# One buffer for the high and low parts of a projection's input, and 512 + 256 column products in place of three of 256

## The chip, the cores and the metric

The kernel runs on one core of one Trainium2 chip. The metric is the time of one execution on the device in microseconds (us). In what follows PE is TensorE (matmuls; PEld its weight loads), DVE is VectorE, ACT is ScalarE, POOL is GpSimd and SP is SyncE, which issues nearly all transfers.

## The reference

Two blocks run one after the other on x, 256 tokens of width 1024, in float32. The first has two layers of a gated mixer and an expert-choice mixture of experts; the change hardly touches it. The second has two layers of this, with `rms` a root-mean-square norm along the tokens' width:

```python
hn = rms(h)
mq, mk, mv, mg, dq, dk, dv, dg, sq, sk, sv, sg = split(hn @ w_in)
#   384 each        256 each         384 each
a = moba(rope(mq), rope(mk), mv)      # 6 heads of 64, causal softmax (one block of 256 keys)
b = diff(rope(dq), rope(dk), dv)      # 8 sub-heads of 32, softmax1 - lam * softmax2, head norm
c = stick(sq, sk, sv)                 # 6 heads of 64, stick-breaking weights, no softmax
h = h + concat(a * silu(mg), b * silu(dg), c * silu(sg)) @ w_out
q = rms(h) @ w_xq                     # 4 heads of 128 against keys and values of a memory
h = h + softmax(q k / sqrt(128)) v @ w_xo
```

## The kernel before

**How a product is made.** Every matrix product of a projection is split: an operand is the sum of a high part (hi, fp32r) and a low part (lo), and the product is hi·wh + hi·wl + lo·wh, summed in PSUM. `wsplit` (L568) makes wh and wl of one weight row block (128 rows): a copy by ACT or DVE into a ring of three wh buffers, a subtraction by DVE or POOL into a ring of three wl buffers. The projection's input stands transposed (features on the partitions) in two SBUF buffers, HH (hi) and HL (lo), each of 8 chunks of 128 features by 256 tokens.

**Two forms of projection.** `linear` (L611) gives tokens on the partitions: the input chunk is the stationary side, wh or wl is streamed (512 or 384 columns). `linear_T` (L626) gives features on the partitions: a 128-column piece of wh or wl is stationary and the 256 tokens of HH or HL are streamed. For each of 8 row blocks kc and each chunk c of 128 output features it issues three matmuls of 256 columns (wh·hi, wl·hi, wh·lo); two chunks share one PSUM bank. In the second block `linear_T` is called five times in a layer: for the stick attention's q, k and g (`stick_in`, L1882, three chunks each), for the moba attention's g (`moba_in`, L1770, three chunks) and for the cross attention's q (`xattn`, L1949, four chunks). That is 16 chunks by 8 row blocks in a layer, 256 such triples in both. (`mem_kv` calls it too, with inputs in G0 and G1; those calls stay as they are.)

**Buffers.** PSUM has eight banks: `lin` three, `aux` four, `acc` one. Scores, transposes and sums of the attentions use `aux`; projections use `lin`. Scratch in SBUF: S2 (five), S4 (three).

**Order of work.** The program is first recorded as a list of operations with their dependencies (`Plan.add`); `Plan.order` then schedules the whole list with fixed costs of its own for each operation and latency, forwards and backwards in eight rounds, and picks the engine where two are allowed (`either`: copies on ACT or DVE, subtractions on DVE or POOL). Each engine then runs its instructions strictly in the order issued. Since everything is issued from one line (`Plan.issue`), all rows of the profile carry the line L461, and the tiles tell them apart. A change of buffers or of operations in `linear_T` therefore moves instructions all over the second block.

**A layer of the second block** issues, in the program's text: norm and transposes into HH, HL (`between_blocks` in layer 0, `norm2` after), `stick_in` (q, k, v, g), `diff_in` (two blocks of 512 columns by `linear`), `stick`, `moba_in` (three blocks of 384 columns by `linear`, then g), `diff`, `moba`, `w_out` by `linear` from XC (hi) and KC (lo), then `xattn`. The schedule runs the attentions of one kind between the projections of the next.

Of the kernel before, what the change touches and what calls it, by code (L numbers as in the profile page):

```python
# [12 lines left out]
F32 = mybir.dt.float32  # L13
F32R = mybir.dt.float32r
# [3 lines left out]
ALU = mybir.AluOpType  # L18
# [18 lines left out]
C_END = C_ROPE + 512  # L37


BUFS = {"W": (2048, 4), "HH": (2048, 1), "HL": (2048, 1), "OH": (2048, 1), "OL": (2048, 1), "Z0": (2048, 1), "Z1": (2048, 1),  # L40
        "QA": (2048, 1), "QB": (1024, 1), "KX": (2048, 1), "KC": (2048, 1), "G0": (2048, 1), "G1": (2048, 1), "XC": (2048, 1),
        "DFT": (2048, 1), "S4": (1024, 3), "S2": (512, 5), "wh": (512, 3), "wl": (512, 3), "gb": (1024, 1),
        "M": (2304, 1),
# [1 line left out]
        "lin": (512, 3), "aux": (512, 4), "acc": (512, 1)}  # L45

PARTS = {"Vx": (0, 512), "Vc": (512, 512), "ropeg": (1024, 512), "kf": (1536, 384), "pr1": (1920, 192), "pr2": (2112, 192)}
SHARED = {"PT": ("Vx", "Vc", "kf")}

MIXED = ("HH", "HL", "OH", "OL", "QA", "QB", "KX", "KC", "DFT", "G0", "G1", "XC")  # L50
PSUM_TAGS = ("lin", "aux", "acc")

O_LF, O_GQ, O_GK, O_GV, O_WQ, O_WK, O_WV, O_GATE = 0, 256, 768, 896, 1024, 1280, 1408, 1536
# [86 lines left out]
class Buffer:  # L140


    def __init__(self, make, row=0, after=None):
        self.make, self.row, self.after = make, row, after
        self.tile = None
        self.seen, self.ops = [], []
# [321 lines left out]
class Net:  # L468
    def __init__(self, tc, A, out, ctx, dbg=None, stop=None):
        self.tc, self.nc, self.A, self.out = tc, Plan(tc.nc), A, out  # L470
        self.dbg, self.stop = dbg or {}, stop
        self.sp = ctx.enter_context(tc.tile_pool(name="g", bufs=1))
        self.pp = ctx.enter_context(tc.tile_pool(name="pp", bufs=1, space=bass.MemoryType.PSUM))
        self.bufs, self.turn = {}, {}
        self.wring, self.wonce = ["W"], []
        self.wseq = 0
        self.loads = []
        self.bg, self.bgrate = [], 0


    def slot(self, tag):

        if tag in SHARED:
            i = self.turn[tag] = self.turn.get(tag, -1) + 1
            return self.slot(SHARED[tag][i % len(SHARED[tag])])
        if tag in PARTS:
            o, n = PARTS[tag]
            return self.slot("M")[:, o:o + n]
        n, count = BUFS[tag]
        i = self.turn.get(tag, 0)  # L490
        self.turn[tag] = i + 1
        psum = tag in PSUM_TAGS
        key = f"{tag}{i % count}"
        old = self.bufs.get(key)
        if old is None or tag in MIXED:
            pool, name = self.pp if psum else self.sp, f"{key}_{i}"
            old = self.bufs[key] = Buffer(lambda: pool.tile([128, n], F32, name=name, tag=key), 0 if psum else n, old)
        return View(old, bass.AP(self.A["consts"].tensor, 0, [[n, 128], [1, n]]))

    def t(self, shape, dt, tag):  # L500
        n = math.prod(shape[1:])
        v = self.slot(tag)[:shape[0], :n]
        if dt != F32:
            v = v.bitcast(dt)
        if len(shape) > 2:
            k = "abcde"[:len(shape) - 1]
            v = v.rearrange("p (%s) -> p %s" % (" ".join(k), " ".join(k)), **dict(zip(k, shape[1:])))
        return v
# [21 lines left out]
    def wslot(self):  # L530
        if self.wonce:
            tag = self.wonce.pop(0)
        else:
            tag = self.wring[self.wseq % len(self.wring)]
            self.wseq += 1
        return self.t([128, BUFS[tag][0] // 1024 * 1024], F32, tag)

    def wload(self, src, k0, nk, c0, ncol):
        t = self.wslot()
# [83 lines left out]
            for t in range(2):  # L623
                evac(t, n0 - c0, ps[t][:, :width])

    def linear_T(self, hi, lo, src, c0, evac, K=8, n=4):  # L626

        nc = self.nc
        ps = [self.lin_ps() for _ in range((n + 1) // 2)]
        ws = self.split_stream(src, [c0], K, list(range(K)), 128 * n)  # L630
        for kc in range(K):
            wh, wl = next(ws)
            for c in range(n):
                o = ps[c // 2][:, (c % 2) * 256:(c % 2) * 256 + 256]
                cs = slice(c * 128, c * 128 + 128)
                st = kc == 0 and c % 2 == 0
                nc.tensor.matmul(o, wh[:, cs], hi[:, kc, :], start=st, stop=False, skip_group_check=True)
                nc.tensor.matmul(o, wl[:, cs], hi[:, kc, :], start=False, stop=False, skip_group_check=True)
                nc.tensor.matmul(o, wh[:, cs], lo[:, kc, :], start=False, stop=kc == K - 1, skip_group_check=True)
        for c in range(n):  # L640
            evac(c, ps[c // 2][:, (c % 2) * 256:(c % 2) * 256 + 256])

    def evac(self, out, ps):
        self.copy(out, ps)
# [61 lines left out]
        self.to_T(xn, a, b, hi, lo)  # L706

    def hilo(self, a, b):
        return self.t([128, 8, 256], F32R, a), self.t([128, 8, 256], F32R, b)

    def sub_scaled(self, out, f, hi, scale):
# [1170 lines left out]
    def stick_in(self, hi, lo, w_in, r, R, vg):  # L1882
        q = self.t([128, 2, 3, 256], F32R, "QA")
        k = self.t([128, 2, 3, 256], F32R, "KX")
        v = vg[:, :768].rearrange("p (t c) -> p t c", t=2)
        g = vg[:, 768:].rearrange("p (c q) -> p c q", c=3)

        def split(dst, scale):
            def ev(c, ps):
                f = self.t([128, 256], F32, "S2")  # L1890
                self.nc.vector.scalar_tensor_tensor(out=f, in0=ps, scalar=scale, in1=R, op0=ALU.mult, op1=ALU.mult)
                self.split_evac(dst[:, 0, c], dst[:, 1, c], f)
            return ev
        self.linear_T(hi, lo, w_in, 2560, split(q, 0.125), n=3)
        self.linear_T(hi, lo, w_in, 2944, split(k, 1.0), n=3)
        self.linear(hi, lo, w_in, 3328, 384, lambda t, n0, ps: self.scaled(v[:, t], ps, r[:, t:t + 1]), width=384)
        self.linear_T(hi, lo, w_in, 3712, lambda c, ps: self.times(g[:, c], ps, R), n=3)
        return q, k, v, g

    def stick(self, q, k, v, g, mh, ml):  # L1900
# [168 lines left out]
```

## Time and profile before

| | |
|---|---|
| median of three runs | 2073.83 us (2080.98, 2073.66, 2073.83) |
| the profiled execution's own time | 2074.04 us |
| its span in the trace | 2072.3 us |
[...]
| PE busy | 1834.5 us (89% of the span) |
| DVE / ACT / POOL busy | 891.8 / 850.4 / 305.0 us |
| HBM traffic | 606.63 MB read, 294 GB/s over the span |
| the second block | from about 1683 us to the end |

The span is measured from the first to the last instruction; the execution's own time is 1.7 us more. The first block and its experts fill the first 1683 us; in the stretches with the experts' weights the transfers run at 421 GB/s. In the second block TensorE is busy nearly all the time.

### The profile page before, as it was taken

How to read it: one execution, taken by the hardware profiler on the slowest of the kernel's cores; microseconds unless marked ns; L12 is line 12 of the kernel's file. 1: busy time of each engine (PE TensorE's matmuls, PEld its weight loads, DVE VectorE, ACT ScalarE, POOL GpSimd, SP SyncE). 2: the span in 40 equal slices, each digit the busy share in tenths (PEclk: the TensorE clock that was granted, in tenths of full speed). 3: DMA queues.
4: the chain of work that ended last, by engine and by line, in shares of the span. 5: the costliest groups of instructions: out<-in, count | busy, mean ns of one | idle time of the engine just before them, and what ended most of it. 6: DMA issues, size and time to landing. Idle time of an engine off the chain costs nothing.

```text
span 2072.3 us, 29481 instructions
## 1 busy us (share of the span) xinstructions
PE 1834.5 (89%) x11564; PEld 1137.8 (55%) x11564; DVE 891.8 (43%) x1862; ACT 850.4 (41%) x1878; POOL 305.0 (15%) x388
## 2 busy tenths in 40 slices
PE   7999999999999898878999997766766689999998
PEld 4666767775443332225676774322322258889887
DVE  3855786682020110206865750101001057767775
ACT  3664666552222221115664541100101046776675
POOL 1302340230000000003501210000000023312521
PEclk9999999999999999999999998777777779999999
DMA  9667573678999999997657889999999975446331
GB/s 341 237 224 264 183 264 122 206 274 296 420 377 421 421 421 421 421 421 272 223 195 258 279 307 417 421 421 421 421 421 421 421 253 163 136 128 181 120 129 65
DMA packets 150347, 611.72 MB, mean 295 GB/s; under 512 B 10144, under 2 KB 32320, under 8 KB 96192
## 3 DMA queue, kind: packets, MB, share of 16 engines
q1 hardware_dynamic: 150208, 609.84, 77.0%
q8 instruction: 91, 1.49, 0.3%
q14 instruction: 48, 0.39, 0.1%
HBM read 606.63 MB, written 3.16 MB: 294 GB/s over the span
## 4 chain that ended last, share of the span: by engine, by line
PE 60%; DMA 27%; DVE 6%; POOL 3%; issue 2%; ACT 2%; SPq 0%; POOLq 0%; DVEq 0%; ACTq 0%
PE lin L461 44%; PE aux L461 13%; DMA W<-w_up_e 5%; DMA G<-w_gate_e 3%; DMA W<-w_gate_e 3%; PE acc L461 2%; DMA M<-w_up_e 2%; DMA Z<-w_gate_e 2%; DMA G<-w_up_e 2%; DMA Z<-w_down_e 2%; DVE S L461 1%; POOL sm L461 1%; DVE wl L461 1%; ACT S L461 1%; DMA OL<-w_down_e 1%
## 5 line engine op out<-in xcount | busy, mean ns | idle before, releaser
L461 DVE TENSOR_TENSOR wl<-W,wh 128x512 fp32r<-128x512 f32 (+1 forms) x504 | 354.8, 708 | 170.1 <-ACT wh L461 166.9
L461 ACT ACTIVATE wh<-W 128x512 fp32r<-128x512 f32 (+1 forms) x457 | 276.6, 608 | 254.3 <-PE lin L461 191.9
L461 DVE TENSOR_TENSOR S<-lin,S 128x512 f32<-128x512 f32 (+1 forms) x32 | 17.9, 558 | 601.1 <-PE lin L461 601.1
L461 POOL TENSOR_TENSOR wl<-W,wh 128x512 fp32r<-128x512 f32 (+1 forms) x72 | 92.5, 1287 | 920.7 <-DVE XC L461 420.2
L461 ACT ACTIVATE S<-lin 32x512 f32<-32x512 f32 (+2 forms) x94 | 52.1, 555 | 399.0 <-PE lin L461 398.2
L461 PE MATMUL lin<-wl,HH 128*128 128x512 f32 (+1 forms) x600 | 206.0, 395 | 3.7 <-DVE wl L461 3.0
L461 PE MATMUL lin<-wh,HL 128*128 128x512 f32 (+1 forms) x600 | 203.5, 391 | 2.8 <-DVE HL L461 1.7
L461 PE MATMUL lin<-wh,HH 128*128 128x512 f32 (+1 forms) x600 | 204.0, 394 | 0.0
L461 PE MATMUL lin<-W,S 128*32 128x256 f32 (+1 forms) x960 | 110.8, 528 | 44.0 <-DMA W<-w_up_e 13.3
L461 PE MATMUL aux<-cst,S 128*128 128x128 f32 x620 | 122.0, 287 | 24.9 <-DVE S L461 18.5
L461 PEld LDWEIGHTS aux<-cst,S 128*128 128x128 f32 x620 | 82.0, 153 | 85.4 <-DVE S L461 40.0
L461 PEld LDWEIGHTS lin<-wl,HH 128*128 128x128 f32 x600 | 108.2, 189 | 33.1 <-DVE wl L461 7.9
L461 PEld LDWEIGHTS lin<-wh,HH 128*128 128x128 f32 x600 | 108.8, 189 | 26.9 <-issue 6.8
L461 PEld LDWEIGHTS lin<-wh,HL 128*128 128x128 f32 x600 | 109.1, 188 | 24.0 <-issue 5.2
L461 ACT ACTIVATE S<-aux 128x512 f32<-128x512 f32 (+4 forms) x134 | 64.7, 489 | 114.1 <-PE aux L461 113.1
L461 PE MATMUL lin<-wh,OL 128*128 128x512 f32 x272 | 95.3, 401 | 1.5 <-DVE OL L461 1.5
L461 PEld LDWEIGHTS lin<-W,S 128*32 128x32 f32 (+1 forms) x960 | 36.9, 137 | 105.2 <-issue 33.3
L461 ACT ACTIVATE S<-aux,sm 128x256 f32<-128x256 f32 (+2 forms) x136 | 71.4, 528 | 28.6 <-DVE sm L461 27.4
L461 ACT ACTIVATE XC<-lin 32x256 f32<-32x256 f32 x60 | 22.5, 374 | 142.7 <-PE lin L461 142.1
L461 POOL TENSOR_SCALAR sm<-sm 128x1 f32<-128x1 f32 (+3 forms) x42 | 17.4, 415 | 423.5 <-ACT G L461 384.1
L461 PE MATMUL lin<-Z,S 128*32 128x256 f32 (+1 forms) x528 | 66.4, 508 | 14.9 <-DMA Z<-w_up_e 7.7
L461 PE MATMUL lin<-wh,OH 128*128 128x512 f32 x208 | 75.8, 404 | 1.5 <-ACT wh L461 1.1
(413 smaller groups left out, 3379.9 us busy)
## 6 DMA issues: line engine op xcount, KB each, us to landing
W<-w_up_e SPq DMA_DIRECT2D x65, 1024.0 KB, 19.0
W<-w_in SPq DMA_DIRECT2D x62, 1024.0 KB, 5.3
W<-w_ada SPq DMA_DIRECT2D x40, 1024.0 KB, 5.0
G<-w_gate_e SPq DMA_DIRECT2D x36, 1024.0 KB, 17.4
W<-w_down_e SPq DMA_DIRECT2D x33, 1024.0 KB, 19.0
Z<-w_gate_e SPq DMA_DIRECT2D x24, 1024.0 KB, 18.1
W<-w_in SPq DMA_DIRECT2D x32, 768.0 KB, 4.7
DFT<-w_gate_e SPq DMA_DIRECT2D x23, 1024.0 KB, 19.8
```

Of the source, the lines that this page charges most:

```text
L461: fn(*(self.real(a) for a in args), **{k: self.real(a) for k, a in kw.items()})
```

## The change

HH and HL become the two halves of one buffer HX (4096 values a partition), so that one access pattern spans the 256 hi and the 256 lo columns of a chunk. `linear_T` then issues, for each row block and output chunk, one matmul of 512 columns (wh against hi and lo) into a whole PSUM bank, and one of 256 columns (wl against hi) into its lower half. The upper half holds wh·lo, and has to be added at the end: a copy of it from PSUM into an S2 buffer (ACT or DVE), and an add by DVE of the lower half. A chunk takes a bank of its own: q of the stick attention and g of the moba attention three `lin` banks, k and g of the stick attention three `aux` banks, q of the cross attention three `lin` and one `aux`.

```diff
-BUFS = {"W": (2048, 4), "HH": (2048, 1), "HL": (2048, 1), "OH": (2048, 1), ...
+BUFS = {"W": (2048, 4), "HX": (4096, 1), "OH": (2048, 1), ...
+HALVES = {"HH": ("HX", 0), "HL": ("HX", 1)}
...
-MIXED = ("HH", "HL", "OH", "OL", "QA", "QB", "KX", "KC", "DFT", "G0", "G1", "XC")
+MIXED = ("OH", "OL", "QA", "QB", "KX", "KC", "DFT", "G0", "G1", "XC")
...
-    def linear_T(self, hi, lo, src, c0, evac, K=8, n=4):
-
-        nc = self.nc
-        ps = [self.lin_ps() for _ in range((n + 1) // 2)]
+    def linear_T(self, hi, lo, src, c0, evac, K=8, n=4, banks=None):
+
+
+        nc = self.nc
+        both = self.both.get(id(hi))
         ws = self.split_stream(src, [c0], K, list(range(K)), 128 * n)
+        if both is None:
+            ps = [self.lin_ps() for _ in range((n + 1) // 2)]
+        else:
+            ps = [getattr(self, (banks or "lin lin lin aux").split()[c] + "_ps")() for c in range(n)]
         for kc in range(K):
             wh, wl = next(ws)
             for c in range(n):
+                cs = slice(c * 128, c * 128 + 128)
+                if both is not None:
+                    nc.tensor.matmul(ps[c], wh[:, cs], both[0][:, :, kc, :], start=kc == 0, stop=kc == K - 1, skip_group_check=True)
+                    nc.tensor.matmul(ps[c][:, 0:256], wl[:, cs], hi[:, kc, :], start=False, stop=kc == K - 1, skip_group_check=True)
+                    continue
                 o = ps[c // 2][:, (c % 2) * 256:(c % 2) * 256 + 256]
-                cs = slice(c * 128, c * 128 + 128)
                 st = kc == 0 and c % 2 == 0
...
         for c in range(n):
-            evac(c, ps[c // 2][:, (c % 2) * 256:(c % 2) * 256 + 256])
+            if both is None:
+                evac(c, ps[c // 2][:, (c % 2) * 256:(c % 2) * 256 + 256])
+                continue
+            f = self.t([128, 256], F32, "S2")
+            self.copy(f, ps[c][:, 256:512])
+            nc.vector.tensor_tensor(out=f, in0=ps[c][:, 0:256], in1=f, op=ALU.add)
+            evac(c, f)
...
     def hilo(self, a, b):
+        if a in HALVES:
+            tag = HALVES[a][0]
+            self.plain.pop(tag, None)
+            v = self.fresh(tag).bitcast(F32R).rearrange("p (a k c) -> p a k c", a=2, k=8)
+            hi, lo = v[:, 0], v[:, 1]
+            self.both[id(hi)] = v, hi
+            return hi, lo
         return self.t([128, 8, 256], F32R, a), self.t([128, 8, 256], F32R, b)
...
         def split(dst, scale):
             def ev(c, ps):
-                f = self.t([128, 256], F32, "S2")
-                self.nc.vector.scalar_tensor_tensor(out=f, in0=ps, scalar=scale, in1=R, op0=ALU.mult, op1=ALU.mult)
-                self.split_evac(dst[:, 0, c], dst[:, 1, c], f)
+                self.nc.vector.scalar_tensor_tensor(out=ps, in0=ps, scalar=scale, in1=R, op0=ALU.mult, op1=ALU.mult)
+                self.split_evac(dst[:, 0, c], dst[:, 1, c], ps)
             return ev
         self.linear_T(hi, lo, w_in, 2560, split(q, 0.125), n=3)
-        self.linear_T(hi, lo, w_in, 2944, split(k, 1.0), n=3)
+        self.linear_T(hi, lo, w_in, 2944, split(k, 1.0), n=3, banks="aux aux aux")
         self.linear(hi, lo, w_in, 3328, 384, lambda t, n0, ps: self.scaled(v[:, t], ps, r[:, t:t + 1]), width=384)
-        self.linear_T(hi, lo, w_in, 3712, lambda c, ps: self.times(g[:, c], ps, R), n=3)
+        self.linear_T(hi, lo, w_in, 3712, lambda c, ps: self.times(g[:, c], ps, R), n=3, banks="aux aux aux")
         return q, k, v, g
```

The rest of the diff is bookkeeping (`fresh`, `slot`, `wslot`: the two halves of HX still serve the first block as HH and HL).

The order of the first block stays as it was but for a few exchanges of neighbours. Three places of the second block are shown. The first is ACT at the start of the second block, layer 0, where it empties the transposes (aux) into the high part and into a scratch S of which the low part is made; x, KC and sm belong to the norm before them, and the S rows of 128x1024 are its sums of squares. Before:

```order
L461 ACTIVATE HH_19_9760<-aux_1_340,sm_3_112 128x256
L461 ACTIVATE S_4_232<-aux_1_340,sm_3_112 128x256
L461 ACTIVATE S_1_544,sm_4_117<-x_64 128x1024
L461 ACTIVATE S_0_525,sm_5_565<-KC_17_9783 128x1024
L461 ACTIVATE HH_19_9760<-aux_1_340,sm_3_112 128x256
L461 ACTIVATE S_0_175<-aux_1_340,sm_3_112 128x256
L461 ACTIVATE HH_19_9760<-aux_2_119,sm_3_112 128x256
L461 ACTIVATE S_1_338<-aux_2_119,sm_3_112 128x256
L461 ACTIVATE HH_19_9760<-aux_2_119,sm_3_112 128x256
L461 ACTIVATE S_2_208<-aux_2_119,sm_3_112 128x256
L461 ACTIVATE S_2_828,sm_5_565<-KC_17_9783 128x1024
```

And with the change, the last pairs of the same work:

```order
L463 ACTIVATE HX_9730<-aux_3_122,sm_3_112 128x256
L463 ACTIVATE S_3_223<-aux_3_122,sm_3_112 128x256
L463 ACTIVATE wh_1_202<-W_1_181 128x384
L463 ACTIVATE HX_9730<-aux_3_122,sm_3_112 128x256
L463 ACTIVATE S_4_231<-aux_3_122,sm_3_112 128x256
L463 ACTIVATE wh_2_205<-W_1_181 128x384
L463 ACTIVATE S_0_524,sm_5_564<-KC_17_9769 128x1024
L463 ACTIVATE S_1_543,sm_4_117<-x_64 128x1024
L463 ACTIVATE S_2_827,sm_5_564<-KC_17_9769 128x1024
L463 ACTIVATE S_0_175<-lin_1_220 128x256
```

The three wide squares moved from between the pairs to behind all eight; the last row is the new copy of q's upper half.

The second place is PE where the stick attention's scores (aux<-QA,KX) begin in layer 0. Before, they follow the end of g (lin<-HH,wh of 256 columns) and one matmul of `diff_in` (512 columns):

```order
L461 MATMUL lin_2_277<-HH_19_9760,wh_2_205 128x256
L461 MATMUL lin_2_277<-HH_19_9760,wl_2_215 128x256
L461 MATMUL lin_2_277<-HL_18_9773,wh_2_205 128x256
L461 MATMUL lin_0_217<-wh_0_200,HH_19_9760 128x512
L461 MATMUL aux_1_340<-QA_6_9925,KX_7_10016 128x256
```

With the change 72 matmuls of `diff_in` stand between g and the scores (56 in layer 1); these are the last of them:

```order
L463 MATMUL lin_2_276<-wl_2_215,HX_9730 128x512
L463 MATMUL lin_0_217<-wl_2_215,HX_9730 128x512
L463 MATMUL lin_2_276<-wh_2_205,HX_9730 128x512
L463 MATMUL lin_0_217<-wh_2_205,HX_9730 128x512
L463 MATMUL aux_3_122<-QA_6_9993,KX_7_10038 128x256
```

So the stick attention starts later against the projections.

The third place is PE at the start of the diff attention, layer 0: its scores are aux<-OL,OH, aux<-trib,identb adds the causal mask, aux<-cst,S are transposes. Before, matmuls of `moba_in` (384 columns) stand between them:

```order
L461 MATMUL aux_3_122<-OL_36_10580,OH_38_10554 128x128
L461 MATMUL lin_2_277<-wh_2_205,HL_18_9773 128x384
L461 MATMUL lin_0_217<-wh_2_205,HL_18_9773 128x384
L461 MATMUL aux_0_177<-OL_36_10580,OH_38_10554 128x128
L461 MATMUL aux_3_122<-OL_36_10580,OH_38_10554 128x256
L461 MATMUL aux_0_177<-OL_36_10580,OH_38_10554 128x256
L461 LDWEIGHTS identb
L461 MATMUL aux_3_122<-trib,identb 128x2x128
L461 MATMUL lin_2_277<-wh_0_200,HH_19_9760 128x384
L461 MATMUL lin_0_217<-wh_0_200,HH_19_9760 128x384
```

With the change:

```order
L463 MATMUL lin_1_220<-wh_1_202,XC_3_10472 128x512
L463 MATMUL lin_2_276<-wh_1_202,XC_3_10472 128x512
L463 MATMUL aux_0_177<-OL_36_10654,OH_38_10616 128x128
L463 MATMUL aux_0_177<-OL_36_10654,OH_38_10616 128x256
L463 LDWEIGHTS identb
L463 MATMUL aux_0_177<-trib,identb 128x2x128
L463 MATMUL aux_3_122<-cst,S_1_337 128x128 x3
L463 MATMUL aux_1_339<-OL_36_10654,OH_38_10616 128x128
L463 MATMUL aux_1_339<-OL_36_10654,OH_38_10616 128x256
L463 LDWEIGHTS identb
L463 MATMUL aux_1_339<-trib,identb 128x2x128
L463 MATMUL aux_3_122<-OL_36_10654,OH_38_10616 128x128
```

`moba_in` has ended by then, and what little stands between the scores is the beginning of `w_out` (lin<-wh,XC). In each layer, from the first diff score to the first moba score, PE has 62 projection matmuls of 384 and 63 of 256 columns before, and 21 of 512 and 3 of 256 with the change; from there to the last value product of moba (acc<-M,G), 9 of 256 and 30 of 512 before, and 12 of 512 with the change.

## Rows read from the trace of the kernel before

**Rows 1.** The page: busy time by engine, GB/s in 40 slices, the chain by engine.

```profile
PE 1834.5 (89%) x11564; PEld 1137.8 (55%) x11564; DVE 891.8 (43%) x1862; ACT 850.4 (41%) x1878; POOL 305.0 (15%) x388
...
GB/s 341 237 224 264 183 264 122 206 274 296 420 377 421 421 421 421 421 421 272 223 195 258 279 307 417 421 421 421 421 421 421 421 253 163 136 128 181 120 129 65
...
PE 60%; DMA 27%; DVE 6%; POOL 3%; issue 2%; ACT 2%; SPq 0%; POOLq 0%; DVEq 0%; ACTq 0%
```

**Rows 2.** Stretches: length, busy PE, PEld, DVE, ACT, POOL (x instructions), clock, DMA share, GB/s.

```profile
1692.60:1697.50 4.90, 4.90 (x23) 4.90 (x24) 3.42 (x9) 1.25 (x3) 1.45 (x3) 0.50 0.68 258
1697.50:1726.40 28.90, 28.74 (x216) 28.39 (x216) 18.90 (x38) 16.70 (x35) 3.08 (x3) 1.00 0.67 196
1726.40:1753.70 27.30, 27.30 (x143) 21.55 (x142) 24.07 (x48) 19.98 (x41) 12.24 (x17) 1.00 0.50 151
...
1776.83:1805.13 28.30, 28.30 (x210) 26.29 (x210) 22.84 (x70) 19.90 (x61) 7.23 (x12) 1.00 0.45 145
1805.00:1824.20 19.20, 18.25 (x130) 12.82 (x128) 15.95 (x47) 16.27 (x52) 3.69 (x6) 1.00 0.29 107
...
1853.80:1867.50 13.70, 12.20 (x78) 10.52 (x77) 8.22 (x22) 11.45 (x33) 0.00 (x0) 1.00 0.20 59
```

**Rows 3.** PE's timeline, each row with its start in us: 256 columns, then 384.

```profile
1717.78 0.28 PE L461 MATMUL lin<-HH,wh 128*128 128x256 f32 x1
...
1726.41 0.39 PE L461 MATMUL lin<-wh,HH 128*128 128x512 f32 x1
...
1778.05 0.34 PE L461 MATMUL lin<-wl,HH 128*128 128x384 f32 x1
...
1778.92 0.34 PE L461 MATMUL lin<-wh,HL 128*128 128x384 f32 x1
```

**Rows 4.** A stretch of 512-column matmuls, columns as in rows 2 without POOL, tile lin alone.

```profile
1728.14:1739.73 11.59, 11.59 (x52) 9.39 (x50) 1.09 (x2) 0.69 (x1) 1.00 0.57 171
```

**Rows 5.** PE's timeline at the start of the second block, with idle time before.

```profile
1683.86 0.38 PE L461 MATMUL lin<-HH,wh 128*128 128x256 f32 x1
...
1692.59 0.58 PE L461 MATMUL lin<-HL,wh 128*128 128x256 f32 x1 [2.94 <-DVE HL L461]
1692.97 0.42 PE L461 MATMUL lin<-HH,wh 128*128 128x256 f32 x1
1693.19 0.41 PE L461 MATMUL lin<-HH,wl 128*128 128x256 f32 x1
```

**Rows 6.** ACT's and DVE's timelines in the same place.

```profile
1685.48 1.09 ACT L461 ACTIVATE S<-x 128x1024 f32<-128x1024 f32 x1
...
1689.34 0.54 ACT L461 ACTIVATE S<-aux,sm 128x256 f32<-128x256 f32 x1
1689.70 1.13 ACT L461 ACTIVATE S<-KC 128x1024 f32<-128x1024 f32 x1
...
1701.04 1.08 DVE L461 SCALAR_TENSOR_TENSOR S<-lin,Z 128x256 f32<-128x256 f32 x3
```

**Rows 7.** DVE's groups by form, first diff score to first moba score, 1776.83 to 1805.13.

```profile
L461 DVE TENSOR_TENSOR wl<-W,wh 128x384 fp32r<-128x384 f32 x16 | 8.9, 559 | 1.3 <-ACT wh L461 1.1
...
L461 DVE TENSOR_REDUCE sm<-aux 128x1 f32<-128x256 f32 x8 | 3.3, 417 | 0.1
...
L461 DVE TENSOR_REDUCE sm<-aux 128x1 f32<-128x128 f32 x8 | 2.1, 283 | 0.3 <-PE aux L461 0.3
...
L461 DVE SCALAR_TENSOR_TENSOR QA<-aux,QA 128x384 fp32r<-128x384 f32 x2 | 1.1, 558 | 0.6 <-ACT QA L461 0.6
```

**Rows 8.** Groups by form around the moba scores, 1805 to 1824.2.

```profile
L461 DVE TENSOR_TENSOR wl<-W,wh 128x512 fp32r<-128x512 f32 x7 | 5.1, 731 | 1.2 <-ACT wh L461 1.1
L461 ACT ACTIVATE wh<-W 128x512 fp32r<-128x512 f32 x8 | 5.1, 638 | 1.2 <-PE lin L461 1.2
```

**Rows 9.** Groups by form in the heads of the cross attention, 1853.8 to 1867.5.

```profile
L461 DVE TENSOR_TENSOR OL<-aux,OL 128x256 fp32r<-128x256 f32 x3 | 1.3, 424 | 2.2 <-ACT OL L461 2.2
...
L461 ACT ACTIVATE OL<-aux 128x256 fp32r<-128x256 f32 x3 | 1.2, 389 | 0.8 <-PE aux L461 0.8
```

More of the change, by code (lines that the diff above doesn't have):

```diff
@@ L37 @@
 C_END = C_ROPE + 512
-BUFS = {"W": (2048, 4), "HH": (2048, 1), "HL": (2048, 1), "OH": (2048, 1), "OL": (2048, 1), "Z0": (2048, 1), "Z1": (2048, 1),
+BUFS = {"W": (2048, 4), "HX": (4096, 1), "OH": (2048, 1), "OL": (2048, 1), "Z0": (2048, 1), "Z1": (2048, 1),
         "QA": (2048, 1), "QB": (1024, 1), "KX": (2048, 1), "KC": (2048, 1), "G0": (2048, 1), "G1": (2048, 1), "XC": (2048, 1),
@@ L474, in __init__ @@
         self.bufs, self.turn = {}, {}
+        self.plain, self.both = {}, {}
         self.wring, self.wonce = ["W"], []
@@ L488, in slot @@
             return self.slot("M")[:, o:o + n]
+        if tag in HALVES:
+            tag, h = HALVES[tag]
+            if tag not in self.plain:
+                self.plain[tag] = self.fresh(tag)
+            n = BUFS[tag][0] // 2
+            return self.plain[tag][:, h * n:h * n + n]
         n, count = BUFS[tag]
@@ L498, in slot, with fresh @@
         return View(old, bass.AP(self.A["consts"].tensor, 0, [[n, 128], [1, n]]))
+    def fresh(self, tag):
+        n = BUFS[tag][0]
+        i = self.turn[tag] = self.turn.get(tag, -1) + 1
+        buf = self.bufs[tag] = Buffer(lambda: self.sp.tile([128, n], F32, name=f"{tag}_{i}", tag=tag), n, self.bufs.get(tag))
+        return View(buf, bass.AP(self.A["consts"].tensor, 0, [[n, 128], [1, n]]))
     def t(self, shape, dt, tag):
@@ L535, in wslot @@
             self.wseq += 1
-        return self.t([128, BUFS[tag][0] // 1024 * 1024], F32, tag)
+        n = BUFS[HALVES[tag][0]][0] // 2 if tag in HALVES else BUFS[tag][0]
+        return self.t([128, n // 1024 * 1024], F32, tag)
     def wload(self, src, k0, nk, c0, ncol):
```

## Prediction

> **What bounds the kernel now.** I read the page first, then windows of the second block, then PE's timeline and what ended its idle time. The page says that PE holds 60% of the chain and transfers 27% [rows 1]; the transfers' part is the stretches at 421 GB/s, which belong to the experts of the first block, where the change moves nothing that counts. So only the last 390 us are in play. There PE is busy for 28.74 of 28.90 us in the feature-major projections, for all of 27.30 us under the stick attention and for all of 28.30 us under the diff attention; it waits a little under moba (18.25 of 19.20) and in the heads of the cross attention (12.20 of 13.70) [rows 2]. The second block is bound by PE's own queue, and DVE and ACT are fitted beneath it. A gain must come from fewer PE microseconds or from the few waits; a loss comes wherever PE's order no longer hides the other engines.
>
> **Part 1: three matmuls become two.** From 1717.78 to 1726.41 PE issues the 72 matmuls of g (8 row blocks, 3 chunks, 3 products): 8.63 us, 0.120 us each [rows 3]. At 512 columns 52 records start within 11.59 us, 51 steps of 0.227 us [rows 4]. A triple costs 3 x 0.1199 = 0.360, a new pair 0.227 + 0.120 = 0.347; 12.5 ns less, 256 times: **-3.2 us**. Bounds: nothing, if the 512 columns with halves 2048 values apart run slower; -9.6 us, if the fixed 12.5 ns of both left matmuls went too. I take the rows, since they are the same shapes at the same clock. [...]
>
> **Part 2: the start of the second block.** PE takes up q at 1683.86 and then stands for 2.94 us until 1692.59 for a low part from DVE; the two steps after it start 0.22 us apart, and the clock is 0.50 until 1697.5 [rows 2, 5]. The cause is ACT: the pairs that empty the transposes are interrupted by wide squares of 1.09 to 1.13 us, the last pair only after 1690.6 [rows 6]. In the new order one square stands first and three behind the last pair (the first place of the order). q's products, evacuated from 1701.04 [rows 6], could then end after 8 x 3 x 0.347 = 8.3 us of work at full clock, begun around 1685.3 because the first wide matmul needs both parts and stands behind all 16 transposes: 1693.6, 7 us earlier. ACT needs 16 emptyings and 3 copies at about 0.36 us, 6.9 us, and does not hold that up; POOL's share of the low parts may. Bounds: -8; -3 (the stall goes, the half clock stays). I take **-6 us**, in layer 0 only. The queue has to wait for the norm's R later, but q's banks no longer do: the new copy and add empty them without R.
>
> **Part 3: evacuations.** 32 copies and 32 adds appear. The nearest rows are ACT's 128x256 out of PSUM at 0.389 us and DVE's at 0.424 [rows 9]: 0.81 us a chunk, 26 us if nothing covered them. The 24 in `stick_in` and `moba_in` I cost at nothing: nine chunks in a stretch like 1697.5 to 1726.4 add 3.3 us to DVE's 18.90 and 2.8 to ACT's 16.70 busy of 28.90 [rows 2], and the banks alternate (q on `lin`, k on `aux`, v on `lin`, g on `aux`), so that a call's evacuation lies under the next call's 8.3 us. Without that cover they cost 24 x 0.81 = 19 us. The eight of the cross attention are in the open: the scores wait for q, and little stands between. One chunk's 0.81 us is exposed, the others follow in a pipe: 1 us a layer, **+2 us** (bounds 0 and 8 x 0.81 = 6.5).
>
> **Part 4: what the order loses.** g on `aux` holds three of its four banks, and the scores of the stick attention need them: they now start 72 (56) wide matmuls later (second place), some 16 us. Everything behind moves later against the projections, and the diff and moba attentions are left without cover (third place). Call A the stretch from the first diff score to the first moba score, 28.30 us, and B the next one, 19.20 us [rows 2]. At 384 columns five steps take 0.87 us, 0.174 each [rows 3]. A holds 62 x 0.174 + 63 x 0.120 = 18.4 us of projection, so 9.9 of attention; B 9 x 0.120 + 30 x 0.227 = 7.9, so 11.3 with its waits. With the change A has 21 x 0.227 + 3 x 0.120 = 5.1 and B 2.7: 15.0 and 14.0 us if PE never waited more than now, 29.0 together. The projections taken out run elsewhere and are not lost; a loss is what A and B take beyond 29.0.
>
> DVE's need in A, from the new order at rows' prices: 16 reductions at 0.417 and 0.283, 5.6; eight products of P, estimated at 0.45, 3.6; five wl of 512 at 0.731, 3.7; four rotations at 0.558, 2.2 [rows 7, 8]; ten adds and products for g's at about 0.42, 4.2; small ones, an estimate, 4. That is 23.3, and since neighbours overlap (three of 0.42 in 1.08 us [rows 6], 0.85) 19.8 busy. Before it was 22.84: sixteen wl of 384, 8.9 us, leave [rows 7], but part of what comes in replaces them. ACT in B: 16.27 less three or so of eight weight copies at 0.638 [rows 8], 14.8. So A cannot be below 19.8 nor B below 14.8 if each stretch keeps its work: 5.6 us lost a layer. Low end: DVE and ACT share out their work over both stretches, each about 30.5 us: 1.5. High end: the busiest engine gets 0.85 of the time, as ACT in B now (16.27 of 19.20) and in the cross attention (11.45 of 13.70) [rows 2]: 23.3 + 17.4 - 29.0 = 11.7. I take 6.5, near the bound by stretches because eight independent heads are in flight, **+13 us** for two layers (3 to 23.4). [...]
>
> **Sum.** -3.2 - 6 + 2 + 13 = +5.8 us on the profiled execution's 2074.04: **2079.8 us**. That execution stands 0.2 us above the median, so the sum is good for the median too. A measurement of this kernel tells apart about 0.5%, 10.4 us: below 2063.5 or above 2084.2.
>
> **The rivals.**
> - *The attentions run bare (slower).* A and B become chains from PE to DVE to ACT and back, at 0.85 of the busiest engine: 2074.04 - 3.2 - 6 + 2 + 23.4 = 2090.2. For it: moba and the cross attention run so already where cover is thin. Against: A holds eight sub-heads and also the last work of `moba_in`. It decides once A takes over 21.5 us in each layer. Chance 0.28.
> - *The cover is enough (a small gain).* DVE and ACT work ahead across A and B, 1.5 us a layer: 2074.04 - 3.2 - 6 + 1 + 3 = 2068.8. For it: PE hides everything in A today. Against: DVE's 19.8 us against 15.0. With part 1 and the start at their low bounds 2060.4. Chance 0.11.
> - *The change does not do what it says:* PE's queue waits for banks or for the low parts from POOL at the start, the clock drops to half as before, and parts 1 and 2 give nothing: 2074.04 + 2 + 13 = 2089. Against: the order frees the low parts earlier. Chance 0.06.
> - *A merge is worth more:* with a third fewer weight loads the two matmuls left lose their fixed part too, -9.6 us in place of -3.2: 2073.4. For it: PEld is busy 28.39 of 28.90 us in these projections [rows 2]. Against: wide and narrow differ in these rows by the columns alone, at one full clock. Chance 0.04. [...]
>
> **How the numbers follow.** The forecast's case has 0.51, at 2079.8, itself between 2073 and 2087; it is within 0.5% in 0.44 and slower in 0.07. The bare attentions give 0.22 slower and 0.06 within, the good cover 0.06 faster and 0.05 within, the third rival 0.04 slower and 0.02 within, the fourth 0.04 within. Faster 0.06, within 0.61, slower 0.33. Range, leaving out one tenth at each end: 2067 to 2092.
>
> **What would show it.** In the new profile: 512 + 256 columns at 0.347 us a pair; no 2.94 us wait near 1692, q evacuated near 1694; A at 21 to 22 us and B at 15 with PE idle there for DVE and ACT; `stick_in` with PE still busy throughout; about 1 us of new wait ahead of the cross attention's scores. I am wrong if A and B together stay below 31 us in each layer, if PE waits in `stick_in`, or if the start takes as long as now.

## The result, and the profile after

The changed kernel takes 2099.01 us, the median of four runs (2096.11 to 2103.53), against 2075.41 of four of the kernel before (2073.66 to 2080.98): a ratio of 1.0112, 95% interval 1.0098 to 1.0125, some 23 us slower. The forecast was 2079.8 us, between 2067 and 2092, and most likely no difference that a measurement can tell; the time lies above that range. The profiled execution took 2096.11 us, its span is 2094.2.

The page of the changed kernel, the lines that answer to [rows 1]:

```profile
PE 1850.2 (88%) x11308; PEld 1136.9 (54%) x11308; DVE 908.5 (43%) x1888; ACT 861.3 (41%) x1911; POOL 312.1 (15%) x393
...
PE 59%; DMA 28%; DVE 6%; ACT 3%; POOL 2%; issue 1%; SPq 0%; POOLq 0%; DVEq 0%; ACTq 0%
```

PE issues 256 matmuls fewer and is busy 15.7 us longer. Stretches show where the time goes. A runs from the first diff score to the first moba score, B from there to the start of the last value product of moba; first both of layer 0, then both of layer 1 (columns as in [rows 2]):

```profile
1796.86:1817.43 20.57, 17.73 (x112) 14.25 (x110) 19.49 (x58) 15.97 (x54) 7.04 (x11) 0.92 0.25 84
1817.43:1836.34 18.91, 15.45 (x97) 10.13 (x97) 10.39 (x33) 13.46 (x47) 3.60 (x6) 0.82 0.00 1
1993.57:2015.15 21.58, 19.18 (x111) 15.54 (x110) 19.93 (x58) 15.95 (x54) 7.16 (x11) 0.84 0.24 79
2015.15:2033.45 18.30, 15.43 (x97) 9.94 (x96) 10.00 (x34) 13.24 (x46) 3.60 (x6) 0.81 0.01 1
```

Before, A and B of layer 0 held 18.4 and 7.9 us of projections, by the prediction's count, at a clock of 1.00 [rows 2]; now they hold 5.1 and 2.7. With no wait beyond those of before A should take 15.0 us, and B, which took 18.61 to the start of its last product, 18.6 - 7.9 + 2.7 = 13.4. They take 20.57 and 18.91, and 21.58 and 18.30 in layer 1: **11.1 and 11.5 us lost**. PE now waits, and its granted clock (a share of full speed), 1.00 before, averages 0.92 and 0.82 in A and B of layer 0, 0.84 and 0.81 in layer 1. What ended most of PE's idle time in A and B of layer 0 (us in total, times, longest):

```profile
PE aux L463 <- ACT S L463: 2.4, 1, 2.4
PE aux L463 <- DVE S L463: 2.1, 2, 1.1
PE aux L463 <- ACT M L463: 1.6, 3, 0.8
```

PE's timeline in B, and a stretch of it with columns as above, show what the longest of these waits leaves behind:

```profile
1819.17 0.95 PE L463 MATMUL aux<-KX,QA 64*128 64x128 f32 x12
...
1822.80 1.08 PE L463 MATMUL aux<-cst,S 128*128 128x128 f32 x3 [2.36 <-ACT S L463]
1823.82 1.94 PE L463 MATMUL aux<-KX,QA 64*128 64x128 f32 x12
```

```profile
1822.80:1826.00 3.20, 3.20 (x17) 2.36 (x18) 1.04 (x4) 3.01 (x10) 0.00 (x0) 0.50 0.00 0
```

The same twelve score matmuls take 0.95 us ahead of the wait, where the granted clock is 1.00 (1819.17 to 1820.10), and 1.94 behind it, where it is 0.50. It is 0.50 up to 1828 and 1.00 again from 1830 us.

The stretches ahead of A come near what their work demands. From the first stick score to the first diff score layer 0 takes 51.90 us in place of 50.10, for 1.9 us more of projections. Three pairs of a wide and a narrow matmul take 1.05 us, as rows of k show:

```profile
1703.11 0.86 PE L463 MATMUL aux<-HX,wh 128*128 128x512 f32 x3
1703.81 0.52 PE L463 MATMUL aux<-HX,wl 128*128 128x256 f32 x3
1704.16 0.86 PE L463 MATMUL aux<-HX,wh 128*128 128x512 f32 x3
```

At the start of the second block the wait of 2.94 us [rows 5] is gone and the clock is 1.00 (1686.32 to 1711.20; before, 0.50 from 1692.60 to 1697.50 [rows 2]), while shorter waits stand in its place: up to the first stick score PE waits for low parts and weights for 4.3 us, against 3.9 before. The first transpose of x, the waits, and the last matmuls of q (lin<-HX,wl) in the changed kernel, where [rows 5] and the first transpose of before below answer to them:

```profile
1686.32 0.33 PE L463 MATMUL aux<-cst,x 128*128 128x128 f32 x1 [0.24 <-DVE x L463]
...
1690.03 0.98 PE L463 MATMUL lin<-HX,wh 128*128 128x512 f32 x3 [0.74 <-DVE HX L463]
...
1695.56 0.97 PE L463 MATMUL lin<-HX,wh 128*128 128x512 f32 x3 [1.06 <-DVE HX L463]
...
1697.79 0.94 PE L463 MATMUL lin<-HX,wh 128*128 128x512 f32 x3 [0.93 <-DVE HX L463]
...
1701.35 0.52 PE L463 MATMUL lin<-HX,wl 128*128 128x256 f32 x3
...
1711.20 0.62 PE L463 MATMUL lin<-wl,HX 128*128 128x384 f32 x2 [1.64 <-POOL wl L463]
```

```profile
1681.32 0.27 PE L461 MATMUL aux<-cst,x 128*128 128x128 f32 x1
```

The copies and adds cost what the rows before gave (0.389 and 0.424 us, [rows 9]):

```profile
L463 DVE TENSOR_TENSOR S<-lin,S 128x256 f32<-128x256 f32 x18 | 7.2, 416 | 2.7 <-ACT S L463 2.7
L463 ACT ACTIVATE S<-lin 128x256 f32<-128x256 f32 x18 | 6.2, 381 | 7.1 <-PE lin L463 7.1
```

The second block, from its first transpose of x, takes 407.9 us where it took 391.0; in this pair of executions the other 5.0 us lie ahead of it, in the first block. The text ahead of the prediction says that the first block's order stayed as it was but for a few exchanges of neighbours. That was wrong: of the scheduler's eight rounds the sixth gives the order of the kernel before, and the seventh that of the changed one, and the two place hundreds of operations of the first block differently.

### The profile page after: what moved, and what is told of

Its sections match the earlier page's. It is cut to its first block, busy times and chain, and to the rows that moved or that the text cites. A ratio compares the mean times of both kernels' runs of the same rounds, so it can differ in the third digit from the quotient of the medians.

```text
span 2094.2 us, 29124 instructions
## 1 busy us (share of the span) xinstructions
PE 1850.2 (88%) x11308; PEld 1136.9 (54%) x11308; DVE 908.5 (43%) x1888; ACT 861.3 (41%) x1911; POOL 312.1 (15%) x393
## 4 chain that ended last, share of the span: by engine, by line
PE 59%; DMA 28%; DVE 6%; ACT 3%; POOL 2%; issue 1%; SPq 0%; POOLq 0%; DVEq 0%; ACTq 0%
PE lin L463 42%; PE aux L463 15%; DMA M<-w_up_e 4%; DMA W<-w_gate_e 3%; DMA W<-w_up_e 3%; DMA G<-w_gate_e 3%; PE acc L463 2%; DMA OH<-w_down_e 2%; DMA Z<-w_gate_e 2%; DMA G<-w_up_e 2%; DVE S L463 2%; ACT S L463 2%; DVE wl L463 1%; POOL sm L463 1%; DMA DFT<-w_gate_e 1%
## 5 line engine op out<-in xcount | busy, mean ns | idle before, releaser
L463 ACT ACTIVATE wh<-W 128x512 fp32r<-128x512 f32 (+1 forms) x471 | 283.3, 605 | 262.1 <-PE lin L463 188.8
L463 PE MATMUL lin<-wh,HX 128*128 128x512 f32 (+1 forms) x1200 | 353.0, 390 | 2.2 <-DVE HX L463 1.2
L463 DVE TENSOR_TENSOR S<-lin,S 128x256 f32<-128x256 f32 (+1 forms) x50 | 25.1, 507 | 605.8 <-PE lin L463 603.1
L463 PEld LDWEIGHTS lin<-wh,HX 128*128 128x128 f32 x1200 | 216.6, 189 | 51.0 <-issue 11.7
L463 ACT ACTIVATE S<-lin 32x512 f32<-32x512 f32 (+2 forms) x112 | 58.3, 527 | 406.8 <-PE lin L463 406.1
L463 PE MATMUL lin<-wl,HX 128*128 128x512 f32 (+1 forms) x600 | 203.3, 394 | 6.7 <-DVE wl L463 4.2
L463 PEld LDWEIGHTS lin<-wl,HX 128*128 128x128 f32 x600 | 108.3, 189 | 35.8 <-DVE wl L463 9.0
L463 PE MATMUL lin<-W,HX 128*64 128x512 f32 x384 | 92.5, 600 | 5.5 <-DMA W<-w_up_e 5.5
L463 PE MATMUL lin<-Z,S 128*32 128x256 f32 (+1 forms) x528 | 69.8, 540 | 15.7 <-DMA Z<-w_up_e 7.5
L463 DVE TENSOR_REDUCE sm<-aux 128x1 f32<-128x256 f32 (+3 forms) x136 | 65.9, 502 | 27.6 <-PE aux L463 24.5
L463 PE MATMUL lin<-wl,OH 128*128 128x512 f32 x208 | 76.9, 408 | 0.5 <-DVE wl L463 0.4
## 6 DMA issues: line engine op xcount, KB each, us to landing
W<-w_up_e SPq DMA_DIRECT2D x65, 1024.0 KB, 19.8
W<-w_down_e SPq DMA_DIRECT2D x33, 1024.0 KB, 19.8
DFT<-w_gate_e SPq DMA_DIRECT2D x23, 1024.0 KB, 19.8
```

Source lines behind the costliest of these rows:

```text
L463: fn(*(self.real(a) for a in args), **{k: self.real(a) for k, a in kw.items()})
```

## The experiments

Nine kernels were made for this. A and B are in us, layer 0 and layer 1; "block" is the profiled execution from the first transpose of x to the end; "projections" are what PE's order holds of them in A and B, at the steps of [rows 3, 4]. "Other order" has the first block's order of the changed kernel; the other eight have that of the kernel before.

| kernel | projections in A, B | A | B | clock in B | block | ratio to before (95%) |
|---|---|---|---|---|---|---|
| before | 18.4, 7.9 | 28.30, 28.30 | 18.61, 18.62 | 1.00 | 391.0 | 1 |
| the change | 5.1, 2.7 | 20.57, 21.58 | 18.91, 18.30 | 0.82, 0.81 | 407.9 | 1.0112 (1.0098 to 1.0125) |
| scratch only | 5.2, 2.7 | 17.69, 17.70 | 19.18, 20.16 | 0.82, 0.75 | 408.5 | 1.0069 (1.0054 to 1.0085) |
| stick merged | 18.4, 7.9 | 28.32, 28.30 | 18.65, 18.63 | 1.00 | 385.7 | 0.9988 (0.9975 to 1.0001) |
| order of before | 5.1, 2.7 | 19.22, 18.98 | 19.49, 18.72 | 0.82, 0.82 | 405.2 | 1.0070 (1.0051 to 1.0090) |
| other order | 18.4, 7.9 | 28.32, 28.30 | 19.31, 19.31 | 1.00 | 393.7 | 1.0030 (1.0019 to 1.0041) |
| no scratch | 18.7, 7.9 | 29.88, 29.90 | 18.48, 18.47 | 1.00 | 387.2 | 0.9986 (0.9974 to 0.9998) |
| moba's g merged | 5.1, 2.7 | 21.37, 18.98 | 18.93, 18.94 | 0.82, 0.82 | 411.4 | 1.0099 (1.0084 to 1.0114) |
| cross attention merged | 18.4, 7.9 | 28.30, 28.30 | 18.62, 18.63 | 1.00 | 390.1 | 0.9997 (0.9988 to 1.0006) |
| clock kept | 5.1, 2.7 | 18.08, 18.00 | 17.51, 17.51 | 1.00 | 399.8 | 1.0051 (1.0033 to 1.0069) |
| all but moba's g | 18.4, 7.9 | 28.30, 28.30 | 18.62, 18.63 | 1.00 | 385.8 | 0.9987 (0.9978 to 0.9996) |

**The question of the first four.** The prediction put the lost cover down to the stick attention's g, which holds three aux banks (theory B). The order suggests another cause (theory S). Moba's g now passes through S2 scratch, three buffers of a ring of five, and `slot` hands a ring out in the program's order. The two turns after g's three go to the gates of diff, and the next three, which are g's own buffers again, to the first three of diff's eight heads. So no head can store its exponentials before moba's g, the last projection of `moba_in`, has left its buffer there, and the order that the scheduler makes has the attentions behind it. In the changed kernel's trace DVE's products that empty these buffers (G<-S,Z) and ACT's exponentials of the diff heads (S<-aux,sm; each head begins with one of 128x128) stand in that order, the third head right behind the third product:

```profile
1797.15 0.72 DVE L463 TENSOR_TENSOR G<-S,Z 128x256 f32<-128x256 f32 x1
...
1798.43 0.42 DVE L463 TENSOR_TENSOR G<-S,Z 128x256 f32<-128x256 f32 x1
...
1799.04 0.35 ACT L463 ACTIVATE S<-aux,sm 128x128 f32<-128x128 f32 x1
...
1801.64 0.41 DVE L463 TENSOR_TENSOR G<-S,Z 128x256 f32<-128x256 f32 x1
...
1802.58 0.38 ACT L463 ACTIVATE S<-aux,sm 128x128 f32<-128x128 f32 x1
```

**Scratch only**: the kernel before, with the detour alone.

```diff
-        self.linear_T(hi, lo, w_in, 1152, lambda c, ps: self.times(g[:, c], ps, R), n=3)
+        def ev(c, ps):
+            f = self.t([128, 256], F32, "S2")
+            self.copy(f, ps)
+            self.times(g[:, c], f, R)
+        self.linear_T(hi, lo, w_in, 1152, ev, n=3)
```

> The kernel before, with one edit: moba's g goes from PSUM into an S2 scratch buffer by a copy and is multiplied from there; no merged matmul, no HX, no bank moved. Theory S (the S2 ring is handed out in the program's order, so the scratch of diff's and moba's heads comes behind moba's g, and these attentions fall behind all of moba's projections): the stretches A and B (first diff score to first moba score, and from there to moba's last value product) hold only about 5 and 3 us of projections, the clock sags there as in the changed kernel, and the time rises by 18 to 24 us. Theory B (the prediction's: the stick attention's g on three aux banks holds its scores back): nothing of that is here, so 0 to +2 us for six copies.

Measured: 2091.21 us against 2076.38, 1.0069, some 14 us slower. Six copies of about 0.4 us, whose targets come from the shared ring, give most of the change's loss, with no matmul merged and no bank moved. A and B of layer 0:

```profile
1795.39:1813.08 17.69, 16.40 (x115) 13.27 (x113) 17.45 (x54) 16.60 (x57) 6.70 (x10) 1.00 0.31 115
1813.08:1832.26 19.18, 14.88 (x97) 9.55 (x96) 11.20 (x35) 13.60 (x48) 3.60 (x6) 0.82 0.00 1
```

The sign and the place are theory S's, theory B is out as the cause; the size is under the 18 to 24 us expected, since in A the clock is 1.00 here (0.92 in the changed kernel) and DVE has less to do (17.45 us, 19.49 in the changed kernel).

**Stick merged**: the changed kernel with `linear_T` merged for the stick attention's q, k and g alone.

```diff
-        both = self.both.get(id(hi))
+        both = self.both.get(id(hi)) if merge else None
...
-        self.linear_T(hi, lo, w_in, 1152, lambda c, ps: self.times(g[:, c], ps, R), n=3)
+        self.linear_T(hi, lo, w_in, 1152, lambda c, ps: self.times(g[:, c], ps, R), n=3, merge=False)
```

(and the same for the cross attention's q.)

> The changed kernel with only the stick attention's q, k and g merged and on their new banks (g on three aux banks); moba's g and the cross attention's q are three matmuls of 256 columns again. Theory S: no scratch before diff's heads is tied to moba's g, so the attentions keep their cover: 2 to 6 us faster than before (144 pairs at 10 ns, and the start of the second block). Theory B: the aux banks of g hold the scores back, the attentions lose their cover, 15 to 22 us slower.

Measured: 2073.80 against 2076.38, 0.9988 with an interval that just reaches 1; in its profile the block is 5.3 us shorter. g stands on three aux banks here and A and B keep their cover: theory B falls, and this part of the change is a gain if anything. Nor do g's banks make the stick attention late: its first score starts 43.4 us after the first transpose of x, against 45.4 before and 58.6 in the changed kernel. With moba's g merged alone (below) it is 47.6, with all merged and no scratch (below) 41.1: the lateness comes only where the stick attention's calls are merged and moba's g goes through the scratch.

**Order of before**: the changed kernel with the sixth round's order.

```diff
-            if best is None or end < best[0]:
+            if r == 5:
```

> The changed kernel, but of the scheduler's eight rounds the sixth is taken, as the kernel before does by itself, in place of the seventh; the second block keeps its projections between the same landmarks, the first block gets the order of before again. Theory F (5 us of the loss are the first block's other order): 4 to 6 us faster than the changed kernel, so 17 to 19 us slower than before. Theory N (the first block's 5 us are the spread between executions): as slow as the changed kernel, 22 to 24 us.

Measured: 2091.99 us, 1.0070, 4 thousandths or some 9 us below the changed kernel's 1.0112 (by the ends of the two intervals 1 to 7 thousandths). More than theory F's 4 to 6: in the profiles the block itself is 2.7 us shorter too, mostly in A, where the clock is 1.00 (0.92 in the changed kernel):

```profile
1790.93:1810.15 19.22, 16.48 (x111) 13.12 (x109) 18.90 (x58) 16.00 (x54) 8.01 (x11) 1.00 0.26 88
1810.15:1829.64 19.49, 16.35 (x97) 10.47 (x97) 10.48 (x34) 13.65 (x47) 3.60 (x6) 0.82 0.00 1
```

**Other order**: the kernel before with the seventh round's order, the same line with `r == 6`.

> The kernel before with the seventh round's order in place of the sixth: its first block runs in the order of the changed kernel, its second block holds the same projections between the same landmarks. Theory F: 4 to 6 us slower than before, all of it before 1215 us. Theory N: within 1.5 us of before.

Measured: 2081.39 against 2076.38, 1.0030, some 6 us slower: the other order costs about what theory F says. Where it costs them is open. In its profile 2.7 us of it are in the second block, which begins at 1685.03 us. With the sixth round's order of the first block, one and the same in both, it began at 1681.10 us in one execution and at 1686.15 in another ("other order", then "order of before" and "clock kept"):

```profile
1685.03 0.33 PE L461 MATMUL aux<-cst,x 128*128 128x128 f32 x1
```

```profile
1681.10 0.33 PE L463 MATMUL aux<-cst,x 128*128 128x128 f32 x1 [0.29 <-DVE x L463]
```

```profile
1686.15 0.33 PE L463 MATMUL aux<-cst,x 128*128 128x128 f32 x1 [0.51 <-DVE x L463]
```

So the 5.0 us between the two profiles above are no measure of the first block's order. The runs of this kernel show what the whole other order costs, and not that the cost lies in the first block.

**No scratch**: the whole change, in the sixth round's order, with moba's g copied to its own place in place of S2.

```diff
-            f = self.t([128, 256], F32, "S2")
+            f = self.t([128, 256], F32, "S2") if into is None else into[:, c]
...
-        self.linear_T(hi, lo, w_in, 1152, lambda c, ps: self.times(g[:, c], ps, R), n=3)
+        self.linear_T(hi, lo, w_in, 1152, lambda c, ps: self.times(g[:, c], ps, R), n=3, into=g)
```

> The changed kernel in full (all five calls merged, the same banks), in the sixth round's order as in the run before, but the upper half of moba's g is copied straight to g's own place and added and multiplied there, so that moba's g takes no S2 scratch. Theory S: A and B hold 18.7 and 7.9 us of projections again, the clock stays at 1.00 there, and A and B take 28 and 19 us; the kernel is 3 to 8 us faster than before (256 pairs at 10 ns, the start of the second block). Theory B, or that the three lin banks of moba's g are the cause: 12 to 17 us slower than before, as the changed kernel in this order.

Measured: 2073.42 against 2075.64, 0.9986. The cover is back, with all five calls merged and three lin banks under moba's g, so the banks of moba's g are not the cause either. The gain of some 3 us is at the lower end of what was expected:

```profile
1775.48:1805.36 29.88, 29.22 (x194) 25.79 (x192) 25.47 (x73) 19.88 (x60) 8.23 (x13) 1.00 0.46 149
1805.36:1823.84 18.48, 17.24 (x122) 12.32 (x121) 16.61 (x49) 16.14 (x52) 5.76 (x7) 1.00 0.25 89
```

A is 1.6 us longer than before: DVE is busy 25.47 of 29.88 us there, and PE waits 0.7.

**Moba's g merged**: the flag of "stick merged" the other way round, moba's g alone.

> The changed kernel with only moba's g merged (three lin banks, scratch in S2); the stick attention's calls and the cross attention's q stay three matmuls of 256 columns. Theory S: the whole loss of the second block is here, 13 to 17 us slower than before, as with the scratch alone. Theory B: the stick attention's aux banks are not touched, so within 2 us of before.

Measured: 2096.70 against 2075.64, 1.0099, some 21 us. The loss of the second block is in this one call. Against "order of before" (1.0070) it lacks the 5 us that the stick attention's calls give back. The scratch alone lacks them too and costs 14 us, with the same order of the first block; the 6 us between these two are not explained in full. In the profiles the block is 2.9 us longer than with the scratch alone, and A of layer 0, at a clock of 0.84 in place of 1.00, 3.7:

```profile
1798.98:1820.35 21.37, 19.02 (x111) 15.33 (x109) 19.62 (x58) 15.99 (x54) 7.06 (x11) 0.84 0.22 80
```

**Cross attention merged**: the same flag, the cross attention's q alone.

> The changed kernel with only the cross attention's q merged (four banks, four copies and adds ahead of its scores). The prediction's part 3: 1 us of open evacuation a layer less 0.3 us for 32 pairs, +1.4 us in all. Rival: the evacuations lie beneath q's last matmuls or the clock-keeping ones, 0 to -1 us.

Measured: 2075.47 against 2075.64, 0.9997 (0.9988 to 1.0006). No difference; the rival holds, and the 1.4 us of the prediction's part 3 lie just beyond the interval's end (1.0006 is 1.2 us).

**Clock kept**: "order of before" with 30 matmuls a layer more, into a free lin bank.

```diff
+                if h == 0:
+                    st["d"] = self.lin_ps()
+                for _ in range(10):
+                    j = nc.last()
+                    nc.tensor.matmul(st["d"][:, 0:256], q[:, 0, h // 2, 0:128], k[:, 0, h // 2, :], start=True, stop=True)
+                    nc.chains.append([j, nc.last()])
```

> The changed kernel in the sixth round's order (as two runs before), with 30 matmuls of 256 columns more in each layer's moba attention, whose result nobody reads; 20 of them stand in PE's queue behind the first four heads' scores, where PE waited 2.4 us for ACT. Theory K (a good part of B's 18 to 19 us is the clock that falls while PE idles, 0.81 there): the clock stays at 1.00 in B, and B takes 1.5 to 3 us less in spite of the added work, so 3 to 6 us faster than that run. Theory L (B is the chain through ACT, whatever PE's clock): B as long or longer, 0 to 3 us slower than that run.

Measured: 2087.07 us, 1.0051 against that kernel's 1.0070, some 4 us less with more work on PE; the intervals overlap (1.0033 to 1.0069, 1.0051 to 1.0090), and in the profiles the block is 5.4 us shorter. A and B of layer 0, and PE where it waited:

```profile
1795.97:1814.05 18.08, 16.78 (x112) 13.07 (x110) 17.44 (x57) 16.52 (x56) 6.93 (x10) 1.00 0.27 93
1814.05:1831.56 17.51, 16.14 (x128) 12.14 (x127) 11.11 (x36) 12.89 (x45) 3.60 (x6) 1.00 0.00 1
```

```profile
1815.94 0.95 PE L463 MATMUL aux<-KX,QA 64*128 64x128 f32 x12
...
1816.97 2.64 PE L463 MATMUL lin<-KX,QA 128*128 128x256 f32 x20
...
1820.42 0.44 PE L463 MATMUL aux<-cst,S 128*128 128x128 f32 x2 [0.52 <-ACT S L463]
1820.79 1.04 PE L463 MATMUL aux<-KX,QA 64*128 64x128 f32 x12
```

B loses 2.0 and 1.2 us with the clock at 1.00: theory K, at the lower end of its range and, in layer 1, under it. A is 1.1 us shorter too, with its matmuls partly in another order; the clock is 1.00 in both, so that isn't its doing. B still takes 17.5 us where 13.4 would be free of waits. PE waits 1.4 of them, for ACT and DVE; the added matmuls take some 3.6 (30 at 0.120), partly in place of waits, and the run doesn't say how much of these 3.6 the chain through ACT and DVE would need anyway.

**All but moba's g**: the merged stick and cross attention calls together, in the sixth round's order.

> The changed kernel with the stick attention's q, k, g and the cross attention's q merged, moba's g as before (three matmuls, no scratch), in the sixth round's order. If the parts add up: the 2.5 us gained by the stick attention's calls alone and the 0.6 us of the cross attention's, 2 to 5 us faster than before, A and B at 28.3 and 18.6 us with the clock at 1.00. If a second tie by scratch hides in the cross attention or the stick attention's calls together: slower than before.

Measured: 2072.08 against 2075.25, 0.9987 (0.9978 to 0.9996), 3 us faster than before and clear of no change. It and "no scratch" are the versions that beat both kernels; the runs don't tell the two apart.

## Why the prediction was wrong, step by step

**What bounds the kernel** was right in the main: PE's queue in the second block, and the loss came where its order no longer hid DVE and ACT. That the change moves nothing in the first block was wrong: its order is another, and the other round's order costs some 6 us as a whole (1.0030), a term that the sum did not have. Which block pays it isn't shown.

**Part 1** held: 0.350 us a pair against 0.360 a triple, 10 ns and 2.5 us in all where 3.2 were forecast.

**Part 2** was right about the clock (1.00 at the start of the block, with no 0.50), not about the waits, and too large. From the first transpose to the last matmul of q PE took at most 19.7 us before (1681.32 to 1701.04, where DVE takes q up [rows 6]) and now takes some 15.4 (1686.32 to the last of three from 1701.35), 4 us less, not 7. q's first wide matmul started 3.7 us after the first transpose, no later than forecast, but two of the next stood 2.0 us for low parts from DVE; then v's first weights come late from POOL (1.64 us), a wait in `stick_in`, one of the prediction's own signs of being wrong. By its work (71 wide matmuls more, 72 pairs for triples) the stretch to the first stick score should have grown from 45.4 to 60.6 us; it took 58.6. Net 2 us gained where 6 were forecast; the merged stick calls alone gain more (5.3 us of the block).

**Part 3** cost nothing that can be measured (0.9997 for the cross attention alone; forecast +2), and the stick attention's 18 evacuations lie beneath PE, as costed. Moba's six, costed at nothing too, carry the scratch on which the loss hangs; done in place they stand in an A that is 1.6 us longer than before ("no scratch").

**Part 4 is the step that failed**, in its cause and in its size. The cause: the lateness of the stick attention behind g's aux banks was named; with the stick's calls merged and moba's g left alone it isn't late and the cover stays, and with the scratch alone, where the stick attention starts as early but for 2.5 us, it goes. What ties diff and moba behind the last projection is three scratch buffers in a shared ring. The size: 13 us were forecast for both layers, 22.6 were lost (21.4 from the prediction's own 29.0, which took B as 19.20 us). DVE's need in A was estimated well, 19.8 us against 19.49 and 19.93 busy (the products of P, put down at 0.45 us without a row, took 0.51 and 0.38 before and take 0.64 and 0.44 now, by width), and A came at 20.6 and 21.6, DVE's own time and little more. B was put at 14.8 by ACT's need, which is 13.46 and 13.24, and takes 18.9 and 18.3: it isn't filled by any engine, it is a chain from scores to exponentials to transposes to products, and the "eight heads in flight" that spoke for a value near the bound don't help once PE has nothing else to issue. Part of that is the clock: behind the 2.36 us wait it is 0.50, and in "clock kept", where it is 1.00, B is 2.0 and 1.2 us shorter in the profiles than in "order of before", with 30 matmuls more. The prediction looked at the clock only at the start of the block.

**The rivals.** The bare attentions had the right picture with 0.28 of the chance: 2090.2 us, against 2091.99 for the change in the sixth round's order. Their price is near in part by luck: it holds 6 us gained at the start, where 2 were, and 2 us for the cross attention, which cost nothing; and their sign, A over 21.5 us in each layer, came in one layer only, as more of the excess is in B. The rest, up to 2099, is the other order. That both came together was in no case, so the range ended too low.

The signs that were named: A at 21 to 22 us with PE idle for DVE was there in layer 1 and nearly in layer 0 (21.58, 20.57), B at 15 was not, and A and B together are 39.5 and 39.9 us, far over the 31 from which the loss begins.

## What to carry to other kernels

A scratch buffer taken from a shared ring is a dependency: whoever gets the next turn waits for it, also where the two share no data. Before a detour through scratch is added, look who takes the ring's next buffers, and write in place where the destination is free anyway. Where an order takes the cover from a chain of engines, cost the chain with its hand-offs, not by the busiest engine, and reckon with a lower clock where PE waits as long as in B here (0.50 behind 2.36 us); and where a global scheduler is in play, compare the order of the parts that the change does not touch as well.

## What the runs showed of the hardware

Beyond what was expected: PE's longest wait was paid for twice here. Behind its 2.36 us the granted clock was 0.50, and the twelve scores took 1.94 us for 0.95. With 30 matmuls a layer whose result nobody reads the clock was 1.00 in A and B, and the block took 399.8 us in place of 405.2 in the profiles; by the runs, 1.0051 against 1.0070 with intervals that overlap, this gain isn't shown. And with one order of the first block the start of the second varied by 5 us between executions (1681.10 and 1686.15), which a comparison of two profiles would have put down to the change.
